# Taking GpSimd's arithmetic out of the token mixer of a hybrid decoder layer

## The chip, the cores and the metric

The kernel runs on one core of one Trainium2 chip. The metric is device time in microseconds (us) of one execution, from the first to the last instruction and what lies around them. Lower is better. The engines are TensorE (PE for its matmuls, PEld for its weight loads), VectorE (DVE), ScalarE (ACT), GpSimd (POOL) and SyncE (SP), which issues all DMAs of the part that matters here.

## The reference

One layer of a decoder: a SwiGLU block (FFN 1), a mixer, a second SwiGLU block (FFN 2). The sequence is 16 meta tokens and 512 real ones, 528 columns in all; the model width is 1024. The mixer runs two token mixers side by side on one projection and adds them under two gates. Cut to what matters (all in float32):

```
P = rmsnorm(h) @ w_in                     # q|k|v, r|k|v, three low-rank inputs, two gates
q, k = rope(q), rope(k)                   # rotary: x1*cos - x2*sin, x2*cos + x1*sin
A = windowed attention(q, k, v)
r, k, v, wd, ad, gd = token_shift_lerp(...)      # p + (prev - p) * mu
w = -softplus(-(w0 + tanh(wd) @ w2)) - 0.5;  decay = exp(-exp(w))
a = sigmoid(a0 + ad @ a2);  g = sigmoid(gd) @ g2
kk = normalised(k * k_k);  k = k * (1 + (a - 1) * k_a)
S = S*decay + (S @ -kk) (kk*a)^T + v k^T;  y = S r      # per head and token
y = groupnorm(y) * lnx_w + lnx_b + sum(r*k*r_k) * v;  R = y * g
h += (sigmoid(G_a) * (A @ W_a) + sigmoid(G_r) * (R @ W_r)) @ W_o
```

## The kernel before, in words

**Matrix products.** Every float32 product is made of three fast ones. `load_w` (L118) brings a 128x512 block of weights (four 128x128 pieces, tile `raw`), ScalarE rounds it to its high part (`whi`, L127), and one engine subtracts to get the low part (`wlo`, L128). `products` (L138 to L140) then multiplies high by high, high by the low part of the activations, and low by high. There are three buffers of `raw`, four of `whi`, four of `wlo`. In the FFNs VectorE makes `wlo`. In the mixer `dense_it` (L347) has GpSimd make it, except for the first three blocks and the two branch products at the end.

**The mixer.** 16 recurrent heads are worked off as 8 pairs j. Each pair goes through five stages, written as generators: `stage_a1` projects k, r, v (`project`), computes sigmoids and norms, the running decay (`tE`, `tsx`) and ends in `a1_end`; `stage_p` forms the chunk operands (tiles `g1e`/`g1o`, `g0`, `kbt`), multiplies them on TensorE into PSUM (`ps`, L770 and L778) and keeps triangles of the results in `gg`, `g1e`/`g1o` and `g3` (printed as `g`); `stage_i` inverts 32x32 triangles, by 31 steps of two VectorE instructions (L836, L838), from the triangles that went to DRAM and back (`Ls`, `LT`, `Xs`); `stage_b` is the recurrence over nine chunks (L894, L895, L902, L903, L904, L907, L913); `stage_t` does the group norm, turns the result round, and applies the gate. Beside them run `qkv` (projection and rotary), `attend`, `gates`, and at the end `att_branch`, `reload` and `rwkv_branch`.

**What sets the order.** `run` (L987) takes one step at a time from the generator with the earliest place on a hand-made timetable (`PLAN`, `LATE`, in units of one pair). A scheduler then orders the instructions of each engine by those priorities and by when it expects operands. The order is fixed in the program: an engine executes its own instructions strictly in that order, and one that waits holds up all that stand behind it.

**What GpSimd does in the mixer.** `wlo` of 100 blocks (L128); the triangle masks (`mask`, L759) on tiles that ScalarE has just copied out of PSUM (L771 to L784); `affine` (L387), which turns tanh(x/2) into a sigmoid; the product that ends `a1_end` (L725); four of the group norm's steps (L928, L935, L947, L948); the low parts of `g2` (L955, L957); the sum and the difference of the rotary (L438, L439); and memsets. No instruction of GpSimd reads PSUM here; ScalarE copies first.

Of the kernel before, what the change touches and what calls it, by code (L numbers as in the profile page):

```python
# [96 lines left out]
def hybrid_layer(ctx: ExitStack, tc: tile.TileContext, a, phases="all"):  # L97
# [228 lines left out]
    def mixer(nm):  # L326
# [20 lines left out]
        def dense_it(src, cuts, M=P, xh=uh, xl=ul, tags=("dn",), eng=nc.gpsimd):  # L347
# [20 lines left out]
        omka = cp.tile([P, 8], F32, name="omka")  # L368
        nc.vector.tensor_scalar(out=omka, in0=vec[:, VEC["ka"]:VEC["ka"] + 8], scalar1=-1.0, scalar2=1.0, op0=OP.mult, op1=OP.add)
# [17 lines left out]
        def affine(x, out=None):  # L387
            nc.gpsimd.tensor_scalar(out=x if out is None else out, in0=x, scalar1=0.5, scalar2=0.5, op0=OP.mult, op1=OP.add)
# [42 lines left out]
        def rotate(x1, x2, c, s, rows, n):  # L431
# [141 lines left out]
        def gates():  # L573
            for i in range(2 * KD):
                for c, pt in dense_it(a["win"][T_G + i], FULL):
# [10 lines left out]
        def att_branch():  # L586
# [7 lines left out]
            for i in range(KD):  # L594
                t = T("gt", SEQ)
                nc.sync.dma_start(out=t, in_=gD[2 * i])
                for c, pt in dense_it(a["wa"][i], [slice(0, SEQ)], P, xh, xl, eng=nc.vector):
# [4 lines left out]
                    nc.sync.dma_start(out=gD[2 * i], in_=t)
                    yield

        def rwkv_branch():

            nm.xh, nm.xl = blocks(up, "uh", KD), blocks(up, "ul", KD)
            for i in range(KD):
# [3 lines left out]
                for c, pt in dense_it(a["wr"][i], [slice(0, SEQ)], P, rh, rl, ("s" if i % 2 else "dn",), nc.vector):  # L612
# [34 lines left out]
        def a1_lora(j, G):  # L647
# [72 lines left out]
        def a1_end(j, G):  # L720
            t2 = G.sq
            nc.scalar.activation(out=t2, in_=G.al, func=AF.Identity, scale=V("ka", j), bias=omka[:, j:j + 1])
            nc.vector.scalar_tensor_tensor(out=G.kn, in0=G.k, scalar=V("kk", j), in1=G.kn, op0=OP.mult, op1=OP.mult)
# [4 lines left out]
        def stage_p(j, G):
# [30 lines left out]
            def mask(dst, base):  # L759

                n = [[0, dst.shape[1]]] if len(dst.shape) == 3 else []
                nc.gpsimd.affine_select(out=dst, in_=dst, pattern=n + [[1, CH]], compare_op=OP.is_ge, fill=0.0, base=base,
                                        channel_multiplier=-1)

            G.Ls = dsc.tile([34, 32, 32], F32, name="Ls")
            late = []
            for h, U, Vr in ((0, LO, HI), (1, HI, LO)):
# [3 lines left out]
                nc.scalar.copy(out=G.g2[U, 0, :], in_=pt[U, Z])  # L771
                mask(G.g2[U, 0, :], -1)
                nc.scalar.copy(out=G.g0[Vr, h, Z], in_=pt[Vr, Z])
                late.append((G.g0[Vr, h, Z], -1))
                for c0 in (1, 5):
# [4 lines left out]
                    nc.scalar.copy(out=G.g2[U, c0:c0 + 4, :], in_=pv[U, :, Z])  # L780
# [3 lines left out]
                    nc.scalar.copy(out=g3[:, c0 - 1:c0 + 3, 1 + h, :], in_=pv[:, :, Y])  # L784
# [135 lines left out]
        def stage_t(j, G):  # L920
# [266 lines left out]
```

## Time and profile before

| | |
|---|---|
| time, median of 3 runs | 1669.98 us (1667.31 to 1674.82) |
| the profiled execution's own time | 1664.78 us |
| its span, first to last instruction | 1662.8 us |
| mean granted TensorE clock | 0.96 |
| TensorE matmuls, busy | 1529.7 us |
| VectorE, busy | 908.8 us |
| ScalarE, busy | 660.9 us |
| GpSimd, busy | 393.4 us |

By the span's own clock FFN 1 lies at about 42 to 420 us, the mixer's pairs at 420 to 1140, the branch products at the mixer's end and the output product at about 1140 to 1245, FFN 2 behind that. A group's row reads: line, engine, operation, tile written <- tiles read, shapes, count | busy us, mean ns of one | idle us of the engine just before them <- what ended most of that idle time. A row of the windows reads: stretch, its length, then busy us and count for PE, PEld, DVE, ACT, POOL, then the granted clock. "Busy" counts an instruction from its start, so time in which a running instruction makes no progress is busy time too.

### The profile page before, as it was taken

Reading aid. Unit: us, or ns where it says so; the run is one execution under the profiler, and the core shown is the slowest. Engines: PE = TensorE matmul, PEld = TensorE weight load, DVE = VectorE, ACT = ScalarE, POOL = GpSimd, SP = SyncE. Lnnn points to the kernel's source line nnn. Section 1 sums busy time; section 2 is a strip of 40 time slices with the busy share of each in tenths; the row PEclk is TensorE's granted clock in tenths of the full one; section 3 lists DMA queues with packets and bytes.
Section 4 is the critical chain, followed back from the end, with each engine's and each line's share of the span. In section 5 each row is a group of like instructions: output and inputs, shape, how many; then the busy total and the mean of one; then the engine's idle time right before and its main releaser. Section 6 shows DMA issues by size and latency. Waiting matters only on the chain.

```text
span 1662.8 us, 26183 instructions
## 1 busy us (share of the span) xinstructions
PE 1529.7 (92%) x9351; PEld 1344.0 (81%) x9351; DVE 908.8 (55%) x2303; ACT 660.9 (40%) x1494; POOL 393.4 (24%) x523
## 2 busy tenths in 40 slices
PE   7999999999959889788888888988999999999997
PEld 7999999998948778677676777766777888888886
DVE  7344433334453677686867686686555444443334
ACT  4333333232423564555545464635334333333221
POOL 3111010001535542544524343520000111110000
PEclk9999999999989898999998798999999999999999
DMA  5333333333323231323222232336743333333332
GB/s 164 91 93 92 89 91 93 106 110 97 107 76 102 75 83 53 84 76 85 70 85 70 76 81 74 85 103 194 231 156 93 92 95 96 95 96 95 95 96 82
DMA packets 137841, 163.25 MB, mean 98 GB/s; under 512 B 56960, under 2 KB 68288, under 8 KB 137712
## 3 DMA queue, kind: packets, MB, share of 16 engines
q1 hardware_dynamic: 137568, 161.54, 33.5%
q8 instruction: 73, 1.20, 0.3%
q14 instruction: 56, 0.46, 0.1%
q10 hardware_dynamic: 144, 0.06, 0.0%
HBM read 140.03 MB, written 21.52 MB: 97 GB/s over the span
## 4 chain that ended last, share of the span: by engine, by line
PE 42%; DVE 12%; DMA 6%; issue 3%; ACT 2%; POOL 2%; SPq 1%; DVEq 0%; POOLq 0%; ACTq 0%
PE dn L138 8%; PE dn L140 8%; PE dn L139 8%; PE pdn L138 3%; PE pdn L139 3%; PE pdn L140 3%; DVE X L838 2%; DVE xtmp L836 2%; DMA LT<-Ls 2%; PE patt L557 2%; DMA Xs<-X 1%; PE py L907 1%; PE small L894 1%; DMA raw<-win 1%; SPq L842 1%
## 5 line engine op out<-in xcount | busy, mean ns | idle before, releaser
L127 ACT CAST whi<-raw 128x512 fp32r<-128x512 f32 (+2 forms) x426 | 259.6, 611 | 596.4 <-PE dn L139 448.5
L138 PE MATMUL dn<-uh,whi 128*128 128x264 f32 (+2 forms) x1192 | 392.7, 330 | 8.8 <-ACT whi L127 6.9
L139 PE MATMUL dn<-ul,whi 128*128 128x264 f32 (+2 forms) x1192 | 390.1, 327 | 1.6 <-DVE ul L177 1.6
L140 PE MATMUL dn<-uh,wlo 128*128 128x264 f32 (+2 forms) x1192 | 391.1, 328 | 0.1
L128 DVE TENSOR_TENSOR wlo<-raw,whi 128x512 fp32r<-128x512 f32 x326 | 222.0, 682 | 296.8 <-ACT whi L127 296.3
L138 PE MATMUL pdn<-uh,whi 128*128 128x264 f32 (+3 forms) x656 | 231.8, 354 | 19.5 <-DVE tv L399 7.1
L138 PEld LDWEIGHTS dn<-uh,whi 128*128 128x128 f32 x1192 | 225.3, 189 | 28.5 <-ACT whi L127 9.4
L139 PEld LDWEIGHTS dn<-ul,whi 128*128 128x128 f32 x1192 | 225.3, 189 | 22.0 <-DVE ul L177 2.2
L140 PEld LDWEIGHTS dn<-uh,wlo 128*128 128x128 f32 x1192 | 225.5, 189 | 21.1 <-DVE wlo L128 0.5
L140 PE MATMUL pdn<-uh,wlo 128*128 128x264 f32 (+3 forms) x656 | 228.4, 349 | 3.0 <-POOL wlo L128 3.0
L139 PE MATMUL pdn<-ul,whi 128*128 128x264 f32 (+3 forms) x656 | 227.7, 348 | 1.3 <-DVE ul L230 1.3
L261 POOL TENSOR_TENSOR sg<-sg,rstd 128x528 f32<-128x528 f32 (+1 forms) x44 | 58.1, 1319 | 530.6 <-ACT sg L260 409.7
L128 POOL TENSOR_TENSOR wlo<-raw,whi 128x512 fp32r<-128x512 f32 x100 | 131.5, 1323 | 142.8 <-ACT whi L127 116.6
L138 PEld LDWEIGHTS pdn<-uh,whi 128*128 128x128 f32 x656 | 130.6, 199 | 33.1 <-DVE tv L399 8.5
L139 PE MATMUL dn<-ml,whi 128*128 128x264 f32 (+2 forms) x478 | 146.5, 306 | 0.0
L138 PE MATMUL dn<-mh,whi 128*128 128x264 f32 (+2 forms) x478 | 146.0, 306 | 0.0
L140 PE MATMUL dn<-mh,wlo 128*128 128x264 f32 (+2 forms) x478 | 145.6, 305 | 0.0
L140 PEld LDWEIGHTS pdn<-uh,wlo 128*128 128x128 f32 x656 | 130.8, 199 | 10.4 <-POOL wlo L128 4.2
L139 PEld LDWEIGHTS pdn<-ul,whi 128*128 128x128 f32 x656 | 131.1, 200 | 8.6 <-DVE ul L230 2.7
L138 PEld LDWEIGHTS dn<-mh,whi 128*128 128x128 f32 x478 | 89.9, 188 | 4.3
L140 PEld LDWEIGHTS dn<-mh,wlo 128*128 128x128 f32 x478 | 90.0, 188 | 4.1
L139 PEld LDWEIGHTS dn<-ml,whi 128*128 128x128 f32 x478 | 89.8, 188 | 3.8
(411 smaller groups left out, 2357.6 us busy)
## 6 DMA issues: line engine op xcount, KB each, us to landing
raw<-win SPq DMA_DIRECT2D x104, 256.0 KB
raw<-w1in SPq DMA_DIRECT2D x88, 256.0 KB
raw<-w2in SPq DMA_DIRECT2D x88, 256.0 KB
raw<-w1out SPq DMA_DIRECT2D x40, 256.0 KB
raw<-w2out SPq DMA_DIRECT2D x40, 256.0 KB
gD<-tgt SPq DMA_DIRECT2D x24, 256.0 KB
raw<-wa SPq DMA_DIRECT2D x16, 256.0 KB
tgt<-gD SPq DMA_DIRECT2D x16, 256.0 KB
```

The lines of the kernel that those rows point to most:

```text
L127: nc.scalar.copy(out=hi, in_=raw)
L128: (eng or nc.vector).tensor_tensor(out=lo, in0=raw, in1=hi.bitcast(F32), op=OP.subtract)
L138: nc.tensor.matmul(o, hi, xh[k][:, c], start=(k == 0), stop=False)
L139: nc.tensor.matmul(o, hi, xl[k][:, c], start=False, stop=False)
L140: nc.tensor.matmul(o, lo, xh[k][:, c], start=False, stop=last)
L261: nc.gpsimd.tensor_mul(out=sg, in0=sg, in1=nm.rstd[:, :n])
L557: nc.tensor.matmul(po[:, x, :], pTs[q][:k1 - k0, P * x:P * x + P], vt[:k1 - k0, q, CH * kv:CH * kv + CH], start=(q == 0), stop=(q == len(p ...
L836: nc.vector.tensor_tensor(out=tmp[:, :n, :w], in0=LT[:, c:c + 1, c + 1:32].to_broadcast([102, n, w]), in1=X[:, :n, c:c + 1].to_broadcast([ ...
L838: nc.vector.tensor_add(out=X[:, :n, c + 1:32], in0=X[:, :n, c + 1:32], in1=tmp[:, :n, :w])
L842: nc.sync.dma_start(out=Xs[:, q:33:3, :], in_=X[34 * q:34 * q + 34])
L894: nc.tensor.matmul(pz[:, U], G.g1[h][:, c - 1, :] if c else G.g0[:, h, :], W[:, c, h, :], start=True, stop=True)
L907: nc.tensor.matmul(py[:, q, h, :], g3[:, c - 1, h, :] if c else G.g3[:, :P], W[:, c, h, :], start=True, stop=True)
```

## The change

All arithmetic of GpSimd inside the mixer goes to other engines; its memsets stay, and so does its multiplication in the FFNs (L261).

- The low parts of the weights in `dense_it`, of `g2`, the rotary's sum and difference, the closing product of `a1_end` and three group-norm steps go to VectorE.
- The masks become products with a 0/1 triangle (`tri`) that VectorE takes straight out of PSUM. ScalarE's 128 copies before them and GpSimd's 160 masks go. Two half-height masks on `g3` become one of full height.
- `affine` goes to ScalarE, and is left in two places only (decay, input of `g2`). For the gates it becomes "plus one" inside VectorE's product that already existed (`scalar_tensor_tensor`), and the factor 1/2 moves into the addition of the output product (`h`). For `a` it becomes "plus one" in `a1_end`, and the 1/2 moves into `hka` and into the product that writes `kbt`.
- The group norm's scale and offset go into ScalarE's copies out of PSUM (L944), which were there already.

The timetable (`PLAN`, `LATE`) is untouched; the scheduler makes a new order from it. Counted over the program, VectorE's list goes from 2305 to 2594 instructions, GpSimd's from 528 to 164, ScalarE's from 1433 to 1323; TensorE's and SyncE's keep their number. The core of the diff:

```diff
-        def dense_it(src, cuts, M=P, xh=uh, xl=ul, tags=("dn",), eng=nc.gpsimd):
+        def dense_it(src, cuts, M=P, xh=uh, xl=ul, tags=("dn",), eng=nc.vector):
...
+        tri = cp.tile([P, 2, CH], F32, name="tri")
+        nc.gpsimd.memset(tri, 1.0)
+        for R in (LO, HI):
+            for q in range(2):
+                nc.gpsimd.affine_select(out=tri[R, q, :], in_=tri[R, q, :], pattern=[[1, CH]], compare_op=OP.is_ge, fill=0.0, base=q - 1,
+                                        channel_multiplier=-1)
...
-        def affine(x, out=None):
-            nc.gpsimd.tensor_scalar(out=x if out is None else out, in0=x, scalar1=0.5, scalar2=0.5, op0=OP.mult, op1=OP.add)
+        def affine(x):
+            nc.scalar.activation(out=x, in_=x, func=AF.Identity, scale=0.5, bias=hb[:x.shape[0]])
...
-            nc.gpsimd.tensor_sub(out=t1, in0=t1, in1=t2)
-            nc.gpsimd.tensor_add(out=t3, in0=t3, in1=t4)
+            nc.vector.tensor_sub(out=t1, in0=t1, in1=t2)
+            nc.vector.tensor_add(out=t3, in0=t3, in1=t4)
...
                     nc.scalar.activation(out=t, in_=t, func=AF.Tanh, scale=0.5)
-                    affine(t)
                     nc.sync.dma_start(out=gD[i], in_=t)
...
-            nc.gpsimd.tensor_mul(out=G.al, in0=G.kn, in1=G.al)
+            nc.vector.scalar_tensor_tensor(out=G.al, in0=G.al, scalar=1.0, in1=G.kn, op0=OP.add, op1=OP.mult)
...
-            def mask(dst, base):
-                n = [[0, dst.shape[1]]] if len(dst.shape) == 3 else []
-                nc.gpsimd.affine_select(out=dst, in_=dst, pattern=n + [[1, CH]], compare_op=OP.is_ge, fill=0.0, base=base,
-                                        channel_multiplier=-1)
+            def masked(dst, src, q):
+                m = tri[slice(0, P) if dst.shape[0] == P else LO, q, :]
+                if len(dst.shape) == 3:
+                    m = m.unsqueeze(1).to_broadcast(list(dst.shape))
+                nc.vector.tensor_mul(out=dst, in0=src, in1=m)
...
-                    nc.scalar.copy(out=G.g2[U, c0:c0 + 4, :], in_=pv[U, :, Z])
-                    mask(G.g2[U, c0:c0 + 4, :], -1)
-                    nc.scalar.copy(out=g1[Vr, c0 - 1:c0 + 3, Z], in_=pv[Vr, :, Z])
-                    late.append((g1[Vr, c0 - 1:c0 + 3, Z], -1))
-                    nc.scalar.copy(out=g3[:, c0 - 1:c0 + 3, 1 + h, :], in_=pv[:, :, Y])
-                    late += [(g3[R, c0 - 1:c0 + 3, 1 + h, :], 0) for R in (LO, HI)]
+                    masked(G.g2[U, c0:c0 + 4, :], pv[U, :, Z], 0)
+                    masked(g1[Vr, c0 - 1:c0 + 3, Z], pv[Vr, :, Z], 0)
+                    masked(g3[:, c0 - 1:c0 + 3, 1 + h, :], pv[:, :, Y], 1)
                     yield
...
-            nc.gpsimd.tensor_tensor(out=yg, in0=yg, in1=spread(s1), op=OP.add)
+            nc.vector.tensor_tensor(out=yg, in0=yg, in1=spread(s1), op=OP.add)
...
-                    nc.scalar.copy(out=yv[U, :, c, :], in_=pv[R, :, x, :])
+                    nc.scalar.activation(out=yv[U, :, c, :], in_=pv[R, :, x, :], func=AF.Identity, scale=V("lw", j)[U], bias=V("lb", j)[U])
...
-            nc.gpsimd.tensor_scalar(out=yc, in0=yc, scalar1=V("lw", j), scalar2=V("lb", j), op0=OP.mult, op1=OP.add)
-            nc.gpsimd.tensor_add(out=yc, in0=yc, in1=bv)
+            nc.vector.tensor_add(out=yc, in0=yc, in1=bv)
```

Where the program's order changes, taken at the third pair's triangles. On GpSimd, before: weight low parts of later blocks and the masks of `stage_p` in one row; the group norm's subtraction (L928) and the closing product of `a1_end` (L725) follow some rows later.

```order
L128 TENSOR_TENSOR wlo<-raw,whi 128x512
L799 MEMSET W 128x128
L762 AFFINE_SELECT gg_7048<-gg_7048 64x256
L762 AFFINE_SELECT g1e<-g1e 64x4x64
L762 AFFINE_SELECT g_7049<-g_7049 64x4x64 x2
L762 AFFINE_SELECT gg_7048<-gg_7048 64x256
L762 AFFINE_SELECT g1e<-g1e 64x4x64
```

After, GpSimd has nothing but memsets there (the line numbers of the changed kernel are a few higher):

```order
L848 MEMSET LT 128x768
L755 MEMSET g1e 64x1024
L755 MEMSET g1o 64x1024
L803 MEMSET W 128x128
L743 MEMSET g_7857 128x256
```

Its weight low parts and masks are now on VectorE.

On VectorE at the same place, before: the end of the inversion (`X`, `xtmp`) interleaved with the chunk operands (`g1e`, `g1o`) and the recurrence's copies (`zy`, `W`).

```order
L836 TENSOR_TENSOR xtmp<-LT,X 102x9x7
L895 COPY zy<-small 128x128
L838 TENSOR_TENSOR X<-X,xtmp 102x9x7
L746 SCALAR_TENSOR_TENSOR g1e<-tkn,tsx 64x8x64
L836 TENSOR_TENSOR xtmp<-LT,X 102x9x6
L750 TENSOR_TENSOR g1e<-tr,tsx 64x8x64
L838 TENSOR_TENSOR X<-X,xtmp 102x9x6
L903 COPY W<-small 64x64
```

After: a weight low part stands ahead of the same pieces.

```order
L842 TENSOR_TENSOR X<-X,xtmp 102x9x7
L128 TENSOR_TENSOR wlo<-raw,whi 128x512
L840 TENSOR_TENSOR xtmp<-LT,X 102x9x6
L756 SCALAR_TENSOR_TENSOR g1e<-tkn,tsx 64x8x64
L842 TENSOR_TENSOR X<-X,xtmp 102x9x6
L899 COPY zy<-small 128x128
L840 TENSOR_TENSOR xtmp<-LT,X 102x9x5
L760 TENSOR_TENSOR g1e<-tr,tsx 64x8x64
```

What moved: `wlo` comes into VectorE's row, and `zy` stands four rows later against the inversion's steps.

On VectorE some ten rows further on, before: the last steps of the inversion, the next recurrence's `zy` and attention's scores (`st`) share the row.

```order
L836 TENSOR_TENSOR xtmp<-LT,X 102x10x2
L895 COPY zy<-small 128x128
L838 TENSOR_TENSOR X<-X,xtmp 102x10x2
L927 TENSOR_SCALAR gs_7653<-gs_7653 128x8
L526 ISA st,mx<-patt,con 128x208
L526 ISA mx 128x1
L836 TENSOR_TENSOR xtmp<-LT,X 102x11
```

After: twelve products out of PSUM nearly in one row, the masks of all four groups of this pair.

```order
L842 TENSOR_TENSOR X<-X,xtmp 102x10x2
L775 TENSOR_TENSOR gg_7013<-ps,tri 64x256
L840 TENSOR_TENSOR xtmp<-LT,X 102x11
L775 TENSOR_TENSOR g1e<-ps,tri 64x4x64
L842 TENSOR_TENSOR X<-X,xtmp 102x11
L775 TENSOR_TENSOR g_7014<-ps,tri 128x4x64
L775 TENSOR_TENSOR gg_7013<-ps,tri 64x256
L775 TENSOR_TENSOR g1e<-ps,tri 64x4x64
L775 TENSOR_TENSOR g_7014<-ps,tri 128x4x64
L775 TENSOR_TENSOR gg_7013<-ps,tri 64x64
L775 TENSOR_TENSOR g_7009<-ps,tri 64x64
```

What moved: the masks stand where the next pair's first `zy` and attention's scores stood; that `zy` is now behind all of them.

More of the change, by code (lines that the diff above doesn't have):

```diff
@@ L367, in mixer @@
         nc.vector.tensor_scalar(out=omm, in0=vec[:, VEC["mul"]:VEC["mul"] + 27], scalar1=-1.0, scalar2=1.0, op0=OP.mult, op1=OP.add)
-        omka = cp.tile([P, 8], F32, name="omka")
-        nc.vector.tensor_scalar(out=omka, in0=vec[:, VEC["ka"]:VEC["ka"] + 8], scalar1=-1.0, scalar2=1.0, op0=OP.mult, op1=OP.add)
+        omka, hka = (cp.tile([P, 8], F32, name=x) for x in ("omka", "hka"))
+        nc.vector.tensor_scalar(out=hka, in0=vec[:, VEC["ka"]:VEC["ka"] + 8], scalar1=0.5, scalar2=None, op0=OP.mult)
+        nc.vector.tensor_scalar(out=omka, in0=hka, scalar1=-1.0, scalar2=1.0, op0=OP.mult, op1=OP.add)
+        hb = cp.tile([P, 1], F32, name="hb")
+        nc.gpsimd.memset(hb, 0.5)
+        tri = cp.tile([P, 2, CH], F32, name="tri")
[4 more added lines that the diff above has]
+                                        channel_multiplier=-1)
         hw0 = cp.tile([P, 16], F32, name="hw0")
@@ L600, in att_branch @@
                         continue
-                    nc.vector.tensor_mul(out=t, in0=t, in1=pt)
+                    nc.vector.scalar_tensor_tensor(out=t, in0=t, scalar=1.0, in1=pt, op0=OP.add, op1=OP.mult)
                     nc.sync.dma_start(out=gD[2 * i], in_=t)
@@ L615, in rwkv_branch @@
                         continue
-                    nc.vector.tensor_mul(out=tr, in0=tr, in1=pt)
+                    nc.vector.scalar_tensor_tensor(out=tr, in0=tr, scalar=1.0, in1=pt, op0=OP.add, op1=OP.mult)
                     nc.vector.tensor_add(out=tr, in0=tr, in1=ta)
@@ L674, in a1_lora @@
                 nc.scalar.activation(out=al[:, c], in_=pt, func=AF.Tanh, scale=0.5, bias=hw0[:, 8 + j:9 + j])
-            affine(al)
             yield
@@ L750, in stage_p @@
                 nc.vector.tensor_mul(out=g1[U, :, kc:kc + CH], in0=chunks(r[U, REAL]), in1=E1r[U, :, 1:65])
-                for src, col in ((bb, bc), (k2, kc)):
-                    nc.vector.tensor_mul(out=KBT[U, 1:, col:col + CH], in0=chunks(src[U, REAL]), in1=E2r[U, :, 1:65])
-                    nc.vector.tensor_mul(out=KBT[U, 0, col:col + NMETA], in0=src[U, 0:NMETA], in1=E2[U, 1:17])
+                for src, col, x in ((bb, bc, 0.5), (k2, kc, 1.0)):
+                    nc.vector.scalar_tensor_tensor(out=KBT[U, 1:, col:col + CH], in0=chunks(src[U, REAL]), scalar=x, in1=E2r[U, :, 1:65],
+                                                   op0=OP.mult, op1=OP.mult)
+                    nc.vector.scalar_tensor_tensor(out=KBT[U, 0, col:col + NMETA], in0=src[U, 0:NMETA], scalar=x, in1=E2[U, 1:17],
+                                                   op0=OP.mult, op1=OP.mult)
                 yield
@@ L770, in stage_p @@
                 nc.tensor.matmul(pt[:, 0:P], KBT[:, 0, :], G.g0[:, h, :], start=True, stop=True)
[L771 to L774, printed above, removed]
+                masked(G.g2[U, 0, :], pt[U, Z], 0)
+                masked(G.g0[Vr, h, Z], pt[Vr, Z], 0)
                 for c0 in (1, 5):
@@ L934, in stage_t @@
             yield
-            nc.gpsimd.tensor_tensor(out=yg, in0=yg, in1=spread(rv), op=OP.mult)
+            nc.vector.tensor_tensor(out=yg, in0=yg, in1=spread(rv), op=OP.mult)
             yield
```

11 lines of the change are left out of this document (4 added, 7 removed).

## The prediction

> **What bounds the kernel now.** I read the page first, then the stages as windows.
>
> ```profile
> PE 1529.7 (92%) x9351; PEld 1344.0 (81%) x9351; DVE 908.8 (55%) x2303; ACT 660.9 (40%) x1494; POOL 393.4 (24%) x523
> PE 42%; DVE 12%; DMA 6%; issue 3%; ACT 2%; POOL 2%; SPq 1%; DVEq 0%; POOLq 0%; ACTq 0%
> ```
>
> ```profile
> core 0: us, PE busy (x) PEld busy (x) DVE busy (x) ACT busy (x) POOL busy (x), PEclk, DMA share, GB/s
> 42.00:420.00 378.00, 374.11 (x3084) 373.63 (x3084) 152.56 (x242) 119.03 (x195) 35.95 (x40) 1.00 0.33 95
> 420.00:1140.00 720.00, 613.91 (x3724) 522.16 (x3723) 485.91 (x1585) 348.82 (x975) 306.29 (x437) 0.91 0.30 84
> 1140.00:1245.00 105.00, 101.98 (x469) 81.39 (x468) 63.59 (x128) 40.43 (x79) 7.32 (x8) 1.00 0.62 196
> 1245.00:1663.00 418.00, 406.59 (x1849) 335.30 (x1847) 177.15 (x306) 131.86 (x214) 28.61 (x22) 0.99 0.33 94
> ```
>
> From 42 us on and outside 420 to 1140 us PE is busy for 97% and more: nothing the change touches has room there. The mixer is another matter: PE is idle for 106 of 720 us (720 - 613.9), its granted clock is 0.91, and DVE is busy for 67%. The chain (second line of the page) runs through PE, DVE and DMA by turns, so here the end is set by latency through several in-order queues, no single engine being full.
>
> Next I looked at who is late when PE idles. One place shows it, by the timeline:
>
> ```profile
> 737.68 3.60 DVE L746 SCALAR_TENSOR_TENSOR g1o<-tkn,tsx 64x512 f32<-64x512 f32 x1
> 738.25 2.48 POOL L128 TENSOR_TENSOR wlo<-raw,whi 128x512 fp32r<-128x512 f32 x2
> 741.55 0.21 DVE L903 COPY W<-small 64x64 f32<-64x64 f32 x1
> 741.79 0.21 ACT L904 COPY W<-small 64x64 f32<-64x64 f32 x1 [2.66 <-DVE W L903]
> ...
> 662.89 0.68 DVE L746 SCALAR_TENSOR_TENSOR g1e<-tkn,tsx 64x512 f32<-64x512 f32 x1
> 663.37 0.95 POOL L745 MEMSET g1o<- 64x1024 f32 x1
> ```
>
> The same instruction takes 0.68 us at 662.89 and 3.60 us at 737.68, where two `wlo` of GpSimd run beside it. Behind it in DVE's queue stands the recurrence's copy L903, behind that ACT's L904, and PE waits for both. Such stalls are counted as DVE's busy time. I compared each DVE instruction of the mixer that lies under an arithmetic instruction of GpSimd with the median of its own shape elsewhere: 138 are over 0.15 us longer, by 92 us together. First and last of the 138:
>
> ```profile
> 420.09 1.38 DVE L401 SCALAR_TENSOR_TENSOR tkn<-tkn,omm,tm 128x256 f32<-128x256 f32 x1 [0.58 <-ACT tm L400]
> ...
> 1118.26 0.57 DVE L308 SCALAR_TENSOR_TENSOR gy<-gt,gy 128x8 f32<-128x8 f32 x1
> ```
>
> So about 19% of DVE's 486 us is standing still (92 / 486), and DVE's own work is some 394 us.
>
> The Trainium skill ("SBUF — State Buffer", section "Who interferes with whom") says that a VectorE instruction with two SBUF inputs contends with a GpSimd instruction that reads SBUF, not with one that only writes. The trace agrees at both places above: full speed beside the memset, a stall of nearly 3 us beside `wlo`. By that rule the memsets that stay on GpSimd cost DVE nothing; if they stalled it too, part of the 92 us would stay.
>
> A cross-check by stretches of 30 us between 540 and 1110 us (19 of them, four shown; PE, PEld, DVE, ACT, POOL):
>
> ```profile
> 600.00:630.00 30.00, 27.39 (x170) 23.37 (x169) 15.72 (x56) 17.67 (x55) 8.31 (x17) 0.90 0.30 79
> 660.00:690.00 30.00, 20.28 (x122) 15.82 (x121) 26.51 (x78) 14.43 (x43) 21.12 (x32) 0.93 0.36 93
> 900.00:930.00 30.00, 21.88 (x145) 18.13 (x143) 20.72 (x61) 16.11 (x49) 14.17 (x23) 0.94 0.34 92
> 1020.00:1050.00 30.00, 27.68 (x142) 23.08 (x143) 23.37 (x97) 12.29 (x36) 8.42 (x12) 0.83 0.25 83
> ```
>
> In the eight with POOL above 14 us PE is idle for 5.7 us on average, in the other eleven for 3.1; sorted by DVE's busy time (above 23 us or below) it is 4.3 and 4.0 us, hardly a difference. 8 x 2.6 = 21 us hang on GpSimd's presence, if that is the cause.
>
> **The change part by part.** First the inversion on DVE, which will be set apart:
>
> ```profile
> L838 DVE TENSOR_TENSOR X<-X,xtmp 102x84 f32<-102x84 f32 (+23 forms) x248 | 77.3, 312 | 3.2 <-DVE W L903 0.2
> L836 DVE TENSOR_TENSOR xtmp<-LT,X 102x84 f32<-102x84 f32 (+23 forms) x248 | 75.8, 306 | 22.9 <-DMA LT<-Ls 9.0 <-DMA raw<-win 5.2 <-DMA X<-xinit 3.6
> ```
>
> The chain by line, in shares of the mixer's 720 us:
>
> ```profile
> by line: DVE X L838 5.3%; DVE xtmp L836 5.2%; PE pdn L138 4.9%; PE pdn L139 4.7%; PE pdn L140 4.6%; DMA LT<-Ls 4.3%; issue 3.8%; PE patt L557 3.7%; DMA Xs<-X 2.6%; PE py L907 2.2%; PE small L894 2.2%; DMA raw<-win 1.9%; SPq L842 1.8%; DMA X
> ```
>
> And the rows for what moves (the second and the last are `wlo` of FFN 1 and of 1100 to 1250 us, on DVE already):
>
> ```profile
> L128 POOL TENSOR_TENSOR wlo<-raw,whi 128x512 fp32r<-128x512 f32 x99 | 130.0, 1322 | 139.9 <-ACT whi L127 113.7 <-issue 5.9 <-PE pdn L140 5.2
> L128 DVE TENSOR_TENSOR wlo<-raw,whi 128x512 fp32r<-128x512 f32 x120 | 82.7, 689 | 132.6 <-ACT whi L127 132.6
> L560 DVE TENSOR_TENSOR ao<-patt,rsum 128x256 f32<-128x256 f32 x16 | 6.7, 418 | 7.1 <-PE patt L557 7.1
> L913 DVE SCALAR_TENSOR_TENSOR W<-py,f,sf 64x64 f32<-64x64 f32 x100 | 28.2, 282 | 22.4 <-PE py L907 20.0
> L784 ACT COPY g<-ps 128x256 f32<-128x256 f32 x32 | 11.8, 369 | 1.3 <-PE py L907 1.0
> L771 ACT COPY gg<-ps 64x64 f32<-64x64 f32 x16 | 3.3, 207 | 8.6 <-PE ps L770 8.3
> L762 POOL TENSOR_SCALAR_AFFINE_SELECT gg<-gg 64x256 f32<-64x256 f32 x32 | 16.8, 524 | 9.6 <-ACT gg L780 6.3 <-PE ps L778 2.3
> L140 PE MATMUL pdn<-uh,wlo 128*128 128x264 f32 (+3 forms) x587 | 202.6, 346 | 3.0 <-POOL wlo L128 3.0
> L128 DVE TENSOR_TENSOR wlo<-raw,whi 128x512 fp32r<-128x512 f32 x40 | 27.8, 695 | 11.2 <-ACT whi L127 10.9 <-issue 0.2
> ```
>
> What DVE gets: 100 `wlo` at 0.689 = 69 us. Masks: per pair 12 of 256 columns out of PSUM, like L560, and 4 of 64, like L913; 8 x (12 x 0.418 + 4 x 0.282) = 49. Two-input products and sums of 512 columns or a little more, at 0.69 like `wlo`: 24 of the group norm, 8 of `a1_end`, 8 of the rotary = 28. The rotary's four smaller ones and `g2`'s 16 low parts: about 6 by the same price per column. Together 152 us. The `kbt`, gate and output products only take another form with the same inputs: nothing. DVE's load is then 394 + 152 = 546 us, against 486 with the stalls. It rises by 60.
>
> What ACT loses: 96 copies at 0.37 and 32 at 0.21 = 42 us. It gains `affine` on the decay, per pair one instruction of 512 columns and one of 16; at twice L784's price and L771's that is 8 x 0.95 = 8 us.
>
> Now what lies on the path. The chain of the whole span holds 12% of DVE, 200 us (of 1662.8), almost all in the mixer, so a DVE microsecond of the mixer is on the path with a share of 200 / 486 = 0.41.
> - Stalls that go: 92 x 0.41 = 38 us.
> - GpSimd's pieces of the chain: 2%, 33 us, go; their successors are counted below as DVE's work. What is late next there is the same DVE queue.
> - ACT's copies before masks: ACT holds 2%, 33 us, of its 349 us in the mixer; 42 x 33 / 349 = 4 us.
> - New DVE work: at most 152 x 0.41 = 62 us, if it is as much in the way as what is there. At least 30: `wlo` off the path altogether (PE waited only 3.0 us for 587 of them) and the other 83 us at DVE's share without the inversion, which is (200 - 10.5% of 720) / (486 - 153) = 0.37. I take a third, 50, nearer to the upper end, since a `wlo` on DVE stands in front of the recurrence whether PE needs it soon or not.
> - New waits in DVE's queue: a `wlo` that stands before its `whi` is ready holds up `zy`, `W` and the masks behind it. On GpSimd 113.7 us of such waiting harmed nobody. The 40 that DVE already makes from 1100 us on waited 11.2 us; 100 of them, 28 us, times 0.41 = 11 at most, 0 if the scheduler puts them late enough. I take 5.
>
> Rotary, FFNs, the tail from 1140 us on: PE is busy there or the stretch is short; nothing. SP issues the same DMAs; `Ls` leaves after one DVE instruction in place of an ACT copy and a mask.
>
> Sum: -38 - 33 - 4 + 50 + 5 = -20 us; with the ends, -45 to -2. On the profiled execution's own 1664.8 us that is 1645. The median of the runs shown is 0.3% higher, 1669.98; there it is 1650, which I forecast. The cross-check, 21 us, falls at the same place.
>
> **The rivals.**
> *VectorE becomes the bound.* In 660 to 690 us DVE is busy for 26.5 of 30 us already. The masks fall into just these stretches, twelve in a row on DVE, where ACT took them off before, and the recurrence's first `zy` stands behind them. If DVE's net load of 60 us comes through whole at the pairs, less the 33 us of GpSimd's pieces, the time is 1670 + 27 = 1697. For it: the added work is all in-order, and the timetable was made for another distribution. Against it: PE's idle time did not follow DVE's load. It decides when the on-path share of the new work passes 75 / 152 = 0.5. The Trainium skill ("Perfetto Trace Analysis", "Optimizing Scalar/DVE Operations") advises to offload work from a saturated VectorE, even to GpSimd, though it adds that between these two it might not help; by the first half this rival wins, by the second the forecast.
>
> *Nothing comes of it.* The stalls were hidden behind DMA (6% of the chain: `Ls`, `Xs`) and PE, and so is the new work: 1670.
>
> *More than forecast.* The 106 us of PE idle time shrinks by half, and the clock rises with it: -53, 1617.
>
> **How the numbers follow.** A measurement of this kernel can tell about 0.5%, 8 us, from no change. The forecast with its ends (1625 to 1668) has 0.45, the greater gain 0.12, nothing 0.13, VectorE as the bound 0.30. Of the forecast's own case some 0.06 lies within 8 us of before (1662 to 1678); of "nothing" 0.11 does, 0.01 lies above and 0.01 below: faster 0.39 + 0.12 + 0.01 = 0.52, same 0.17, slower 0.31. The range 1615 to 1697 leaves out the far ends of the first and last case. The likeliest case's own range is 1625 to 1668.
>
> **What would show it.** Right: DVE's L836, L838, L746, L306 keep one duration per shape; DVE's busy time between 520 and 570 us in the mixer; PE's idle time below 90 us there; POOL off the chain. Wrong: DVE waits of microseconds before `wlo` or the masks with PE idle behind them, more PE idle than 106 us, `zy` late after a row of masks, or DVE instructions still stretched.

## The result and the profile after

The changed kernel takes 1616.84 us (median of 4 runs, 1613.03 to 1621.72); the kernel before took 1668.64 us beside it (1665.04 to 1674.82). The ratio is 0.9687, with a 95% interval of 0.9646 to 0.9729: 52 us faster, where 20 were forecast. The profiled execution took 1614.77 us, its span is 1613.0. Busy times of the engines and the chain that ended last, from the page:

```profile
PE 1512.3 (94%) x9351; PEld 1331.7 (83%) x9351; DVE 939.4 (58%) x2592; ACT 633.6 (39%) x1384; POOL 103.8 (6%) x159
PE 76%; DMA 9%; DVE 9%; ACT 2%; issue 2%; SPq 1%; DVEq 0%; POOL 0%; ACTq 0%
```

Both kernels run the same 9351 matmuls. PE's busy time falls from 1529.7 to 1512.3 us, by 17, at a mean granted clock of 0.97 in place of 0.96; the rest of the span, in which PE is idle, falls from 133 to 101 us, by 32. Together that is the 50 us of span. The chains can't be set side by side share by share: the shares of the one of before add up to 68% of its span, since it can't be followed back beyond 513 us, those of after to 99%.

The same stretches as windows; the mixer's pairs now end some 40 us earlier, so the stretch is 680 us long:

```profile
420.00:1100.00 680.00, 603.75 (x3741) 514.95 (x3739) 520.72 (x1874) 325.11 (x874) 25.36 (x77) 0.93 0.32 91
1100.00:1200.00 100.00, 98.61 (x453) 79.06 (x453) 61.44 (x125) 37.47 (x71) 0.00 (x0) 1.00 0.62 197
```

PE is idle for 76 us (680 - 603.75) in place of 106, at a clock of 0.93 in place of 0.91. VectorE is busy for 521 us of 680, before for 486 of 720. Its groups between 420 and 1140 us:

```profile
L128 DVE TENSOR_TENSOR wlo<-raw,whi 128x512 fp32r<-128x512 f32 x117 | 79.2, 684 | 17.9 <-ACT whi L127 16.4 <-DMA qD<-pT 0.4 <-ACT W L908 0.2
L842 DVE TENSOR_TENSOR X<-X,xtmp 102x84 f32<-102x84 f32 (+23 forms) x248 | 53.8, 217 | 2.1
L775 DVE TENSOR_TENSOR gg<-ps,tri 64x256 f32<-64x256 f32 (+1 forms) x48 | 16.9, 352 | 1.4 <-PE ps L787 0.5
L756 DVE SCALAR_TENSOR_TENSOR g1o<-tkn,tsx 64x512 f32<-64x512 f32 x8 | 5.5, 690 | 0.2
```

One step of the inversion (`X`) takes 217 ns where it took 312: nearly a third of it was standing still. `g1o` has one duration again (all eight take 690 or 691 ns). Each VectorE instruction under GpSimd's arithmetic is compared with the median of its own shape, as in the prediction, but with every excess counted, also below 0.15 us, and from 420 us to the mixer's last recurrence product. By this count stalls go from 100 us to 0, and VectorE's work without them from 407 to 537 us.

### The profile page after: what moved, and what is told of

Same layout as the page of the kernel before. It is cut to its first block, busy times and chain, and to the rows that moved or that the text cites. A ratio compares the mean times of both kernels' runs of the same rounds, so it can differ in the third digit from the quotient of the medians.

```text
span 1613.0 us, 25818 instructions
## 1 busy us (share of the span) xinstructions
PE 1512.3 (94%) x9351; PEld 1331.7 (83%) x9351; DVE 939.4 (58%) x2592; ACT 633.6 (39%) x1384; POOL 103.8 (6%) x159
## 4 chain that ended last, share of the span: by engine, by line
PE 76%; DMA 9%; DVE 9%; ACT 2%; issue 2%; SPq 1%; DVEq 0%; POOL 0%; ACTq 0%
PE dn L140 16%; PE dn L139 16%; PE dn L138 16%; PE pdn L140 5%; PE pdn L138 5%; PE pdn L139 5%; DMA LT<-Ls 4%; DMA Xs<-X 2%; PE py L911 1%; PE patt L569 1%; DVE wlo L128 1%; PE small L898 1%; PE small L906 1%; PE patt L536 1%; PE ps L787 1%
## 5 line engine op out<-in xcount | busy, mean ns | idle before, releaser
L128 DVE TENSOR_TENSOR wlo<-raw,whi 128x512 fp32r<-128x512 f32 (+2 forms) x426 | 289.1, 681 | 308.7 <-ACT whi L127 306.8
L138 PE MATMUL pdn<-uh,whi 128*128 128x264 f32 (+3 forms) x656 | 223.9, 344 | 11.6 <-ACT uh L229 8.4
L140 PE MATMUL pdn<-uh,wlo 128*128 128x264 f32 (+3 forms) x656 | 223.4, 342 | 5.3 <-DVE wlo L128 5.3
L139 PE MATMUL pdn<-ul,whi 128*128 128x264 f32 (+3 forms) x656 | 221.9, 339 | 0.2 <-DVE ul L230 0.2
L138 PEld LDWEIGHTS pdn<-uh,whi 128*128 128x128 f32 x656 | 126.1, 193 | 26.1 <-ACT uh L229 10.8
L140 PEld LDWEIGHTS pdn<-uh,wlo 128*128 128x128 f32 x656 | 127.4, 195 | 13.0 <-DVE wlo L128 7.4
L139 PEld LDWEIGHTS pdn<-ul,whi 128*128 128x128 f32 x656 | 126.4, 193 | 8.8 <-DVE ul L230 2.3
L261 POOL TENSOR_TENSOR sg<-sg,rstd 128x528 f32<-128x528 f32 (+1 forms) x44 | 58.1, 1320 | 603.4 <-ACT sg L260 418.4
L262 DVE TENSOR_TENSOR m<-sg,dn 128x528 f32<-128x528 f32 (+1 forms) x44 | 30.6, 696 | 71.2 <-PE dn L140 67.9
```

Of the source, the lines that this page charges most:

```text
L128: (eng or nc.vector).tensor_tensor(out=lo, in0=raw, in1=hi.bitcast(F32), op=OP.subtract)
L138: nc.tensor.matmul(o, hi, xh[k][:, c], start=(k == 0), stop=False)
L139: nc.tensor.matmul(o, hi, xl[k][:, c], start=False, stop=False)
L140: nc.tensor.matmul(o, lo, xh[k][:, c], start=False, stop=last)
L261: nc.gpsimd.tensor_mul(out=sg, in0=sg, in1=nm.rstd[:, :n])
L262: nc.vector.tensor_mul(out=vw(m), in0=vw(sg), in1=vu)
```

## The experiments

Each kernel ran beside the kernel before on the same chip. Times are medians; ratios are to before. Where an expectation speaks of theory A, it is the prediction's mechanism (GpSimd's reads stall VectorE).

| run | what it is | us | ratio (95%) |
|---|---|---|---|
| e1 | after, useless reads on GpSimd | 1679.98 | 1.0101 (1.0054 to 1.0147) |
| e2 | after, useless writes on GpSimd | 1616.41 | 0.9716 (0.9675 to 0.9758) |
| e3 | after, useless work on VectorE | 1670.25 | 1.0029 (1.0004 to 1.0054) |
| e4 | after, `wlo` back on GpSimd | 1606.46 | 0.9653 (0.9614 to 0.9693) |
| e5 | before, only the masks changed | 1632.16 | 0.9806 (0.9763 to 0.9850) |
| e6 | after, masks back on GpSimd | 1601.78 | 0.9625 (0.9584 to 0.9667) |
| e7 | before, one entry of the timetable | 1659.84 | 0.9974 (0.9947 to 1.0001) |
| e8 | after, the same entry | 1615.80 | 0.9717 (0.9667 to 0.9767) |
| e9 | before, only `wlo` on VectorE | 1602.79 | 0.9633 (0.9605 to 0.9662) |
| e10 | after, `wlo` and masks back | 1627.98 | 0.9812 (0.9755 to 0.9869) |
| e11 | e6 with a bare wait on GpSimd | 1607.57 | 0.9666 (0.9630 to 0.9701) |
| e12 | e6 with `zy` on ScalarE | 1590.36 | 0.9566 (0.9532 to 0.9600) |
| e13 | e9, GpSimd's queue filled, few reads | 1606.99 | 0.9676 (0.9619 to 0.9734) |
| e14 | e9, GpSimd's queue filled with reads | 1634.79 | 0.9827 (0.9772 to 0.9882) |
| e15 | before, in the order of e9 | 1635.02 | 0.9808 (0.9774 to 0.9842) |
| e16 | e9, in the order of before | 1644.38 | 0.9867 (0.9822 to 0.9912) |
| e17 | after, in the order of before | 1665.14 | 1.0010 (0.9988 to 1.0033) |
| e18 | before, in the order of after | 1665.25 | 1.0014 (0.9989 to 1.0039) |

What TensorE did in the profiled execution of nine of them, in us over the whole span (single executions, which lie up to 9 us from the medians above):

| | span | PE busy | PE idle | mean granted clock |
|---|---|---|---|---|
| before | 1662.8 | 1529.7 | 133.1 | 0.960 |
| after | 1613.0 | 1512.3 | 100.7 | 0.970 |
| e1 | 1686.5 | 1554.6 | 131.9 | 0.950 |
| e2 | 1611.6 | 1516.4 | 95.2 | 0.970 |
| e3 | 1666.9 | 1558.5 | 108.4 | 0.942 |
| e13 | 1603.8 | 1506.1 | 97.7 | 0.978 |
| e14 | 1641.5 | 1526.0 | 115.5 | 0.967 |
| e17 | 1665.6 | 1530.8 | 134.8 | 0.955 |
| e18 | 1664.7 | 1543.5 | 121.2 | 0.951 |

The work of PE is the same 9351 matmuls in all nine, and its busy time goes with the granted clock, from 1506.1 us at 0.978 to 1558.5 at 0.942. So these kernels lose time in two ways, by PE's idle time and by a lower clock.

### Prices: reads, writes, and VectorE's own work (e1, e2, e3)

All three add useless instructions beside each weight block of the changed kernel. To make room for the tile `idle`, these kernels (and e13 and e14) have some of the mixer's buffers only as long as the columns that are used.

```diff
-                        w.append(load_w(src[:, KW * q:KW * q + KW, :], KW, M, eng))
+                        w.append(load_w(src[:, KW * q:KW * q + KW, :], KW, M, eng)); eng is None and beside(w[q][0])
...
+        def beside(hi):
...
```

e1 has GpSimd subtract 256 columns of `whi` from themselves, four times; e2 has it do so with 8 columns and write four memsets of 256; e3 is e1's subtraction, twice, on VectorE.

> The changed kernel, with four useless subtractions of 256 columns on GpSimd beside each of the mixer's 100 weight blocks (both inputs in SBUF, result never read): some 280 us of reading work, what GpSimd had before. The order on TensorE, VectorE, ScalarE and SyncE is that of the changed kernel, row for row. Theory A (the gain comes from stalls that GpSimd's reads put on VectorE): the stalls come back, 60 to 110 us of longer VectorE instructions, and the time rises by 30 to 55 us, to 1647 to 1672. Theory B (the gain comes from the new order, from shorter hops and from ScalarE's lighter load; the stalls were mostly hidden): VectorE's instructions are longer as well, but the time rises by less than 10 us.

> As the run with reading work, but beside each block GpSimd does one subtraction of 8 columns and four memsets of 256 columns: the same places, some 130 us of work that only writes. Same order on the four other engines. Theory A: VectorE's instructions keep their lengths, the time stays within 5 us of 1617. A third theory (any work of GpSimd holds VectorE up, reading or not): stalls as in the reading run, in proportion, and 15 us or more.

> The changed kernel with two useless subtractions of 256 columns on VectorE beside each of the mixer's 100 weight blocks: 200 x 0.39 = 78 us more work in VectorE's queue, needed by nobody. It measures the share with which new VectorE work lies on the path, which the prediction put at one third (bounds 0.20 and 0.41). By the prediction: 78 x 0.33 = +26 us (16 to 32). If new work mostly falls into VectorE's idle time, as the chain after the change suggests: under +12 us. The scheduler makes another order for it, so a few us of that may be the order's.

What they add, and a step of the inversion beside it, from the groups between 420 and 1140 us, of e1:

```profile
L375 POOL TENSOR_TENSOR idle<-whi 128x256 f32<-128x256 f32 x396 | 298.1, 753 | 275.2 <-ACT whi L127 248.6 <-POOL tm L410 0.3
L847 DVE TENSOR_TENSOR X<-X,xtmp 102x84 f32<-102x84 f32 (+23 forms) x242 | 72.7, 301 | 2.0
```

of e2:

```profile
L375 POOL MEMSET idle<- 128x256 f32 x392 | 122.3, 312 | 22.0
L847 DVE TENSOR_TENSOR X<-X,xtmp 102x84 f32<-102x84 f32 (+23 forms) x248 | 53.9, 217 | 2.1
```

and of e3:

```profile
L375 DVE TENSOR_TENSOR idle<-whi 128x256 f32<-128x256 f32 x196 | 81.3, 415 | 0.7
```

With reads on GpSimd a step of the inversion takes 301 ns again, with writes 217. e1 takes 63.6 us more than e2, for 90 us more of stalls by the count above (94 against 4): 0.71 for each. The 81.3 us on VectorE cost 53.8 against e2: 0.66 for each (the expectations of e12 and e14 reckon with 0.7 to 0.85). Both prices are well above the prediction's 0.41 and one third: e1 came out above the range of theory A, e3 above the 16 to 32 us by the prediction. e1 left the order of the other engines as it was; e3 did not, so its price has some order in it.

The table above splits these prices. From e2 to e1 PE's idle time grows by 36.7 us, which is 0.41 for each of the 90 us of stalls, the share that the prediction took from the chain; the other 38.2 us between the two executions are PE's own busy time, longer at a clock of 0.950 in place of 0.970. From e2 to e3 idle time grows by only 13.2 us and busy time by 42.1. Most of the price of VectorE's added work is thus a lower clock of TensorE, not PE waiting longer. What lowers the clock these runs don't show.

### One part of the change at a time (e4, e5, e6, e9, e10)

```diff
-        def dense_it(src, cuts, M=P, xh=uh, xl=ul, tags=("dn",), eng=nc.vector):
+        def dense_it(src, cuts, M=P, xh=uh, xl=ul, tags=("dn",), eng=nc.gpsimd):
```

This line makes e4 out of after, and read backwards e9 out of before. e6 is after with the old `mask` and ScalarE's copies, e5 is before with `masked` and `tri`, e10 has e4's line and e6's masks together.

> The changed kernel with one thing undone: the low parts of the mixer's weights go back to GpSimd (100 x 1.32 us there, 69 us off VectorE). Theory A: about half of GpSimd's reading work is back, so half or more of the stalls, 40 to 60 us on VectorE, for 69 us of work less: VectorE's busy time hardly changes, and the time rises by 10 to 30 us. Theory B: VectorE's queue is 69 us lighter and the stalls are hidden, so the time stays or falls.

> The kernel before with one part of the change: the triangle masks as VectorE's products out of PSUM, without ScalarE's 128 copies and GpSimd's 160 masks (weights, group norm, sigmoids and rotary stay on GpSimd). The last four runs say that VectorE's load costs nearly its full length in the changed kernel, and that the weights alone are no gain; so the gain must lie in shorter paths. Theory B1 (the masks' path, copy then mask, was the brake): most of the gain, 1610 to 1630 us. Theory B2 (the order that the scheduler happened to make was the brake): near 1665 or anything within 20 us of it. Theory C (many hops of GpSimd, each worth a little): in the middle, 1635 to 1650.

> The changed kernel with the masks as before: ScalarE copies out of PSUM, GpSimd masks; everything else of the change stays. VectorE loses 49 us of work and gets back the stalls of the masks (at most some 30 us). Theory B1: most of the gain is lost, 1640 to 1665 us. Theory C: 1620 to 1640. If only VectorE's load counted: 1600 or less.

> The kernel before with one part of the change: the subtractions that make wlo go to VectorE, everything else (copies and GpSimd masks, group norm, affine) stays on GpSimd. VectorE gets 70 us of instructions, GpSimd loses some 74 us and all its waits for whi. Theory H (GpSimd's own queue: wlo waits at its head for ScalarE's whi, 113.7 us in before, and masks, group norm and affine stand behind it; taking either the weights or the masks away ends that): 1615 to 1630 us, -35 to -50 against before. Theory C (each piece of GpSimd work costs a little, in proportion to its 290 us, and nothing else): 74 of 290 us of the 69 us or so that GpSimd's pieces cost is -18, and the new VectorE load takes some of it back: 1640 to 1660. The prediction's own prices (GpSimd's wait harmed nobody) put it within 10 us of before.

> The change without its two largest parts: wlo and the masks (ScalarE copy, then GpSimd mask) are again as in before; only group norm, affine with the sigmoid's sums, the rotary sums and g2 are moved off GpSimd. GpSimd keeps some 220 of 290 us. Theory H: the head of GpSimd's queue still waits for whi with the masks behind it, so it stays near before, 1640 to 1665. Theory C: the 69 us go in proportion, 216/290 of them stay, so about -17 us, less what VectorE's added work costs: 1645 to 1660; the two differ little here, but H falls if it comes out at 1620 or less, which would say that the group norm and affine on GpSimd were what cost.

Moved alone, `wlo` gives about 61 us, the masks 32, the rest 31: together over twice what the whole change gives. The two pairs that were tried give 58 (e4) and 62 (e6), more than all three. No sum of fixed prices does that; but each of these kernels also has an order of its own. Few expectations were met: e4 fell where theory A had it rise by 10 to 30 us, e5 lies between the ranges of B1 and C, e6 is below both, and e9 and e10 came out below the ranges of both theories that were set against each other in them.

### GpSimd's queue: waits and time (e11, e13, e14)

e11 adds to e6 one subtraction of 8 columns of `whi` per block, so that GpSimd waits for `whi` where `wlo` stood, ahead of the masks:

```diff
+            nc.gpsimd.tensor_tensor(out=idle, in0=x, in1=x, op=OP.subtract)
```

e13 adds to e9 the same and three memsets of 256 columns, about as long as a `wlo` was; e14 adds to e9 two subtractions of 256 columns of `whi`.

> The fastest kernel so far (the change with the masks back on GpSimd, 1601.78 us) plus one GpSimd subtraction of 8 columns beside each weight block, which reads whi and therefore waits for ScalarE's copy at the place in GpSimd's queue where wlo stood; the result is used by nobody, and the work is some 100 very short instructions. Theory H: the wait alone brings the loss back: the masks stand behind it, 1612 to 1645. Theory C: without the work there is no cost, within 5 us of 1602.

> The kernel before with only wlo on VectorE (1602.79 us), plus useless work on GpSimd in the place of wlo: beside each weight block a subtraction of 8 columns that waits for whi, and three memsets of 256 columns, some 1.3 us together, as long as wlo's 1322 ns was. The order of PE, VectorE, ScalarE and SyncE is that of the kernel with only wlo moved; GpSimd's queue is as full as before, but its added work hardly reads. If the time and the place that wlo takes in GpSimd's queue is what costs (masks, group norm and affine behind it): 1625 to 1650. If the stalls of VectorE under GpSimd's reads are what costs: within 8 us of 1603.

> The same with two useless subtractions of 256 columns of whi beside each weight block in place of the memsets (some 1.5 us a block, 150 us in all, their result is used by nobody): GpSimd's queue as full, and it reads again. Stall theory: VectorE's stalls go from 41 us to about 100, and at the 0.7 to 0.85 us per us that added VectorE time cost in the runs with useless work, 1602.79 + 40 to 55, so 1643 to 1658. Queue theory: as e13, 1625 to 1650, and no more than 10 us above e13.

From the groups between 420 and 1140 us, of e13:

```profile
L374 POOL MEMSET idle<- 128x256 f32 x298 | 93.1, 312 | 16.1
L374 POOL TENSOR_TENSOR idle<-whi 128x8 f32<-128x8 f32 x99 | 39.1, 395 | 166.4 <-ACT whi L127 156.9 <-ACT f L720 7.2
L844 DVE TENSOR_TENSOR X<-X,xtmp 102x84 f32<-102x84 f32 (+23 forms) x248 | 61.6, 248 | 1.5
```

and of e14:

```profile
L374 POOL TENSOR_TENSOR idle<-whi 128x256 f32<-128x256 f32 x200 | 156.7, 783 | 182.7 <-ACT whi L127 166.6 <-ACT f L720 5.2 <-DMA raw<-win 1.3
L844 DVE TENSOR_TENSOR X<-X,xtmp 102x84 f32<-102x84 f32 (+23 forms) x248 | 67.4, 272 | 1.5
```

A wait of 157 us and 132 us of work (93.1 + 39.1) in GpSimd's queue ahead of masks and group norm cost e13 0.0043 of the time against e9, 7 us, with intervals that overlap; e11's wait alone costs as little against e6 (0.0041), less than theory H had and a little more than C's 5 us. That was my theory after e6, and it falls. Reads in the same place cost e14 28 us against e13 (1634.79 - 1606.99), for 44 us more of stalls (88 against 44): 0.63 for each. That is more than the 10 us that the queue theory allows and less than the stall theory's 1643 to 1658. PE's idle time has 17.8 us of it (0.40 for each), its busy time the rest. The scheduler also moved a few rows: about 1% of PE's matmuls stand elsewhere than in e13.

### The order, held fixed (e7, e8, e15, e16, e17, e18)

An early try at the order changed one entry of the timetable.

```diff
-... "stage_t": -265, "stage_p": -66, "stage_i": -182}
+... "stage_t": -265, "stage_p": -60, "stage_i": -182}
```

> The kernel before with one number of the timetable changed slightly (the lateness of stage_p, -66 to -60). Nothing is computed differently; only the order of some instructions changes, about an eighth of VectorE's rows. It sizes what an order is worth by chance. Theory B2: 10 us or more away from 1666. B1 and C: within 8 us.

> The changed kernel with the same number of the timetable changed (-66 to -60). Theory B2: 10 us or more away from 1617. B1 and C: within 8 us.

It moved the time by 0.3% at most, and I dropped the order as a cause; too early. The four later kernels carry a list of instructions per engine, and each instruction on it is tied behind the one listed before it, without a wait. What isn't on the list finds its place by the scheduler. In the traces all 9351 matmuls of e17 stand in the order of before, all those of e18 in the order of after.

```diff
         hybrid_layer(tc, args)
+        pin(tc, nc)
...
+            if prev is not None:
+                tc.add_manual_dep(i, prev.name, mybir.DependencyInfo(mybir.DependencyClass.NoSync, mybir.DependencyReason.DATA), reason="pin")
+            prev = i
```

> The kernel before, same instructions on the same engines (wlo on GpSimd), but the order on PE, VectorE, ScalarE and SyncE is fixed to the one that the scheduler made for the kernel with wlo on VectorE. If the new order is what gives (order theory): 1600 to 1625, most of the 59 us. If the place of wlo is what gives (its stalls and its engine): 1640 to 1665, and 32 us of the 59 is what the reads were seen to cost.

> The kernel with only wlo on VectorE (1602.79 us with its own order), with the order on PE, ScalarE, SyncE and of VectorE's other instructions fixed to that of the kernel before. Order theory: 1640 to 1670, VectorE's stalls halved (about 40 us) and the time near before all the same. Place theory: 1600 to 1625.

> The changed kernel, each instruction on its new engine, with the order of PE and SyncE, and of all VectorE and ScalarE instructions that both kernels have, fixed to that of the kernel before; only the moved instructions find their places anew. If the 52 us come from the place of the work alone: 1610 to 1625. If the order has a share as large as it had for wlo alone (32 to 39 us): 1640 to 1660.

> The kernel before, each instruction on its old engine, with the order of PE and SyncE, and of all VectorE and ScalarE instructions that both kernels have, fixed to that of the changed kernel. If the 52 us come from the place of the work alone: 1655 to 1675. If the order has a share of 32 to 39 us: 1625 to 1637.

| | in the order of before | in the order made for the new places |
|---|---|---|
| nothing moved | 1.0000 | 0.9808 (e15) |
| `wlo` moved | 0.9867 (e16) | 0.9633 (e9) |
| nothing moved | 1.0000 | 1.0014 (e18) |
| the whole change | 1.0010 (e17) | 0.9687 (after) |

For `wlo` alone the place gives 1.3% and the order 1.9%, which add up to 3.2 of the 3.7% of e9. For the whole change neither the place in the old order nor the order at the old places changes the time, and the two together give 3.1%. The expectations had set "place alone" against "order": e15 lies between the two ranges, e16 in that of the order, e17 above both, e18 in that of the place, which e17 rules out. The windows of the mixer, of e17:

```profile
420.00:1140.00 720.00, 611.10 (x3694) 521.55 (x3692) 520.08 (x1859) 318.88 (x855) 25.20 (x77) 0.90 0.29 83
```

and of e18:

```profile
420.00:1140.00 720.00, 626.13 (x3698) 532.22 (x3697) 473.26 (x1579) 345.08 (x956) 303.77 (x437) 0.89 0.29 84
```

e17 has lost GpSimd's arithmetic and still leaves PE idle for 109 us (720 - 611.1), as before did. e18's unchanged time is a balance of two things: PE is idle for 94 us (720 - 626.13) in place of 106, but its clock is 0.89 in place of 0.91, and over the whole span it is busy for 14 us longer and idle for 12 us less than in before. So the new order alone does shorten PE's waits, and the lower clock takes the gain back. Where PE waits, by PE's groups in the same stretch, of before:

```profile
L138 PE MATMUL pdn<-uh,whi 128*128 128x264 f32 (+3 forms) x587 | 205.3, 351 | 18.3 <-DVE tv L399 7.1 <-ACT uh L229 5.4 <-DVE tr L399 2.6
L907 PE MATMUL py<-W,g 128*128 128x64 f32 x260 | 47.5, 280 | 19.0 <-DVE W L903 17.2 <-ACT W L904 1.7
```

of after:

```profile
L138 PE MATMUL pdn<-uh,whi 128*128 128x264 f32 (+3 forms) x638 | 218.4, 345 | 10.8 <-ACT uh L229 8.4 <-DVE tv L411 1.3 <-ACT tal L685 0.3
L911 PE MATMUL py<-W,g 128*128 128x64 f32 x288 | 53.5, 284 | 6.6 <-DVE W L907 5.0 <-ACT W L908 1.2
```

of e17 (lines some 20 higher), with VectorE's masks, and `X`, which no longer stalls:

```profile
L160 PE MATMUL pdn<-uh,whi 128*128 128x264 f32 (+3 forms) x587 | 203.7, 348 | 24.3 <-DVE tgt L614 7.2 <-ACT uh L251 6.8 <-DVE tv L433 4.6
L933 PE MATMUL py<-W,g 128*128 128x64 f32 x256 | 48.2, 285 | 14.6 <-DVE W L929 12.7 <-ACT W L930 1.3
L797 DVE TENSOR_TENSOR gg<-ps,tri 64x256 f32<-64x256 f32 (+1 forms) x48 | 16.9, 353 | 12.6 <-PE ps L809 10.2 <-PE ps L803 1.2 <-PE pt L890 0.6
L864 DVE TENSOR_TENSOR X<-X,xtmp 102x84 f32<-102x84 f32 (+23 forms) x248 | 54.2, 218 | 2.6
```

and of e18:

```profile
L929 PE MATMUL py<-W,g 128*128 128x64 f32 x252 | 49.2, 298 | 15.3 <-DVE W L925 13.3 <-ACT W L926 1.9
L860 DVE TENSOR_TENSOR X<-X,xtmp 102x84 f32<-102x84 f32 (+23 forms) x248 | 80.6, 325 | 2.7
```

The recurrence's product (`py`) waits for VectorE's `W` for 17.2 us before and 5.0 after. Take away the stalls and move the work, in the old order (e17), and 12.7 remain; give the new order alone (e18) and 13.3 remain. Ahead of the projection (`pdn`) PE idles for 18.3 us before, 10.8 after and 24.3 in e17. In e17 one new wait can be named: VectorE stands at the head of its queue for 11.4 us (10.2 + 1.2) until PE has made the products `ps` that it is to mask, after only for 0.5. In before the first reader of `ps` was a copy of ScalarE, and that wait was ScalarE's (its 8.3 us before one such copy stand in the prediction's rows). In the order made for the changed kernel `ps` is there in time.

### A better mixture (e12)

e12 takes e6, the change with the masks left on GpSimd, and moves the recurrence's copy `zy` to ScalarE.

```diff
-                nc.vector.tensor_copy(out=zy[:, q % 2], in_=pz.rearrange("p (h t) -> p h t", h=2))
+                nc.scalar.copy(out=zy[:, q % 2], in_=pz.rearrange("p (h t) -> p h t", h=2))
```

> A candidate: the change with the masks back on GpSimd (1601.78 us), and the recurrence's copy of its product from PSUM (18.6 us on VectorE) moved to ScalarE. If VectorE's load sets the mixer's time at about 0.85 us per us, as the added subtractions showed, 1583 to 1592. If VectorE's queue no longer sets it once the masks are off it, within 5 us of 1602; if the copy then stands behind ScalarE's weight copies, slower than 1605.

The mixer's window of e12:

```profile
420.00:1100.00 680.00, 624.55 (x3888) 530.60 (x3887) 492.69 (x1712) 392.84 (x1094) 112.00 (x238) 0.95 0.34 99
```

PE is idle for 55 us (680 - 624.55), and the ratio, 0.9566 (0.9532 to 0.9600), is the lowest of all. The time lies in the first of the expected ranges, but its order is its own too, and was not held fixed, so the 10 us gained over e6 are not split between the copy's place and the order.

## Why the prediction was wrong, point by point

**What it read rightly.** The mixer is where the time went: some 40 of 50 us of span. The stalls are real, come from GpSimd's reads and not from its writes (e1, e2), and are gone. (For the writes the prediction's own place says little, since the memset at 663.37 us begins 0.2 us before that VectorE instruction ends; e2 says it.) VectorE's work grew by 130 us without stalls (152 forecast), its busy time of 521 us and PE's idle time of 76 lie inside the stated signs, POOL is off the chain. "On GpSimd 113.7 us of such waiting harmed nobody" holds: e11 and e13 put such waits back at 0 to 7 us.

**The step that failed** is the sum: "-38 - 33 - 4 + 50 + 5 = -20 us". Every term in it prices an instruction that goes or comes in the order of before, as that trace showed it. Held to that order the change gives nothing: e17 measured 1.0010 (0.9988 to 1.0033), -2 to +5 us. The 52 us appear only where the new places and the order that the scheduler made for them come together; that order alone gives nothing either (e18: 1.0014). For the new order the sum has no term, and none for the granted clock: 17 of the 50 us of span are PE's shorter busy time and not shorter waits. The scheduler enters the text once, in the +5 for new waits in VectorE's queue ("0 if the scheduler puts them late enough"). The rows shown as moved were priced only for the harm in them.

**Two terms were mis-sized as well, in opposite directions.** A stalled microsecond is worth 0.63 to 0.71 (e14, e1) and not 0.41: 92 x 0.67 is -62, not -38. The share from the chain, 0.41, was right for PE's idle time (0.40 and 0.41); it left out PE's longer busy time at the lower clock. (The chain reaches back to 513 us only, so it misses 93 us of the mixer; over the stretch that it covers the share is about the same.) A microsecond of new VectorE work cost 0.66 in e3, whose order is its own, and not a third: 152 x 0.66 is +100, not +50. With these the prediction's own sum, its other terms unchanged, is -62 - 33 - 4 + 100 + 5 = +6 us, close to what e17 measured. That doesn't confirm them: they were measured in other orders, and for `wlo` alone in the old order they fail. In e16 stalls fall by 61 us (100 to 39 by the same count) and VectorE gets 69 us of `wlo`, which makes -41 + 46 = +5 us; measured were some 22 us less than before.

**The rivals.** "VectorE becomes the bound" was to decide when the share of new work passes 0.5. In e3 it did pass it, yet the loss of 27 us didn't come, in the old order (e17) or the new one. "More than forecast" gave the right time, 1617, and was right that both PE's idle time and the clock would move. It put the whole gain down to idle time shrinking by half, though; over the span that shrank by 32 of 133 us, and the other 17 us are busy time, which goes with the clock. That the number fits so well is in part luck.

**What stays open.** Which rows of the new order matter is not shown. The wait for `ps` is one sign of them, 11.4 us of VectorE's time in e17. What sets the granted clock, and why the new order lowers it at the old places (0.951, e18) and not at the new ones (0.970), is open. Why place and order add up for `wlo` alone and need each other for the whole change was not tested. The fixed order covers only instructions that both kernels have; the moved ones were placed by the scheduler in e17 and e18 too, perhaps badly. No kernel was tied to its own order, so a cost of the tie itself is not excluded; e15 and e16 carry the same tie and are faster than before.

## What to carry to other kernels

Where a scheduler orders the program, moving an instruction to another engine is two changes: the price of the move at the old order, which the trace of before can show, and a new order for everything else, which it can't. Here neither gave anything alone, and both together gave 52 us, so a range must leave room for the order in both directions. Tie the instructions of one build into the order of the other to tell the two apart, before giving the work's new place the credit. Split each difference into PE's idle time and PE's busy time: with the same matmuls the second went with the granted clock in all nine kernels of the table. When several engines are close to the path, try the parts apart: here both pairs of parts that were tried beat all three.

## What the runs showed of the hardware

A GpSimd subtraction of 256 columns takes 753 to 783 ns, while memsets of 256 columns take 312 and leave VectorE at full speed (e2: 122 us of them, `X` at 217 ns). The masks, which GpSimd reads and writes in place, stall VectorE far less than `wlo`: with only the masks there (e6) the count of stalls is 14 us for 85 us of GpSimd's work, with only `wlo` (e4) 61 us for 135. One kernel, in one order, can take times 22 us apart as the granted clock differs: the four executions of e10 go from 1617.28 us at a mean clock of 0.978 to 1639.51 at 0.960. A bare wait in GpSimd's queue, 301 us in e11, costs nothing that could be told apart (0.0041 against e6, with intervals that overlap):

```profile
L376 POOL TENSOR_TENSOR idle<-whi 128x8 f32<-128x8 f32 x100 | 42.7, 427 | 338.0 <-ACT whi L127 301.3 <-ACT f L724 20.9 <-DMA aD<-ao 15.3
```
